# First fixed expert without a split, blocks of up to 32 slots on column quarters, in a two-layer mixture-of-experts encoder

## The chip, the cores and the metric

The kernel runs on one core of one Trainium2 chip. The metric is the device time of one execution of the whole program in microseconds, given as the median of several runs. Engines are named as in the profile: PE is TensorE's matmul, PEld its weight load, DVE is VectorE, ACT is ScalarE, POOL is GpSimd, SP is SyncE, which issues most DMAs.

## The reference

Two post-norm residual layers over 1024 tokens of width 1024. Each layer has a mixer (attention) and then the mixture of experts that the change is about: 4 groups of 8 experts, each token goes to its best group and there to its best two experts.

```python
for i in range(DEPTH):                      # DEPTH = 2
    m = even_mixer(x, ...) if i % 2 == 0 else odd_mixer(x, ...)
    x = layer_norm(DN_ALPHA * x + m, ln1_g[i], ln1_b[i])
    f = hier_moe(x, w_router_group[i], ..., w_gate[i], w_up[i], w_down[i])
    x = layer_norm(DN_ALPHA * x + f, ln2_g[i], ln2_b[i])

# in hier_moe, for the tokens xb of an expert e, w their gates:
hdn = jax.nn.silu(xb @ w1[e]) * (xb @ w3[e])      # 1024 -> 512, twice
y = (hdn @ w2[e]) * w[:, None]                    # 512 -> 1024
```

All is float32.

## The kernel before

**Experts in an order.** Each layer works through 32 experts one after the other (`moe`, the loop over `s`; position `p` in `ex.order`). Positions 0 and 1 are "fixed": experts 0 and 1, whatever their load, so that their weights can be loaded before the router has chosen (`NFIX = 2`). The other 30 are ranked by load, and `ROOM` gives each rank `r` its slots: ranks 0 to 3 ("big") a block of 128 slots and a remainder of 48, 40, 32 and 16; ranks 4 to 13 ("mid") one block of up to 128; ranks 14 to 29 ("light") 64 down to 24 slots. Fixed experts are ranks 30 and 31, 128 slots each. `light(p)` tells whether a position is of the light kind. In the order, rank 2 stands at position 18, rank 3 at 24, and the four light ranks with 32 or 24 slots at 27, 29, 30 and 31, the end.

**Two kinds of block.** A 128-slot block is computed with split operands: every weight piece (128x1024, half of a 1 MB load) is split into `hi` (ACT, line 2052) and a remainder `lo` (DVE, line 2056, or for the two fixed experts often POOL, line 2054), and each product is three matmuls (`mm3`, lines 169 to 171). Twelve pieces make an expert; five pairs of buffers hold them (`PIECES`). `fill` splits up to `AHEAD` = 3 pieces beyond the one in use; line 825 calls `ex.fill(3)` already during the output projection of the mixer. A 64-slot block takes the loaded weights as they are: `pair` (line 1148) issues two matmuls with 64 stationary columns each, gate and up (or the two halves of down), on the two column halves of the array (line 1151). The trace has two matmul records for each such float32 matmul.

**One stage `s`.** For `i` in 0 to 7 gate and up of expert `s`, then for `i` in 8 to 11 down of expert `s - 1`. In between stand: `deliver(s - 2)` (gate times result plus the gathered token, line 1203, DVE), `turn_hidden(s - 1)` (transposes of the hidden values, line 1181; for 64-slot blocks also silu and the product, lines 1188 and 1189), `scatter` and `gather` (indirect DMAs from POOL, lines 1209 and 1120), and at `i == TURN` (6) `turn(s + 1)`, the transposes of the next expert's tokens (lines 1133 to 1142). In stage 0 one step of `route_rest` (slot tables from one-hot matmuls, lines 1023 to 1062) follows each `i`; the rest of it, `decode` (lines 1071 to 1081) and `gather(2)` come at `i == 0` of stage 1.

**Loads.** Each expert is six loads of 1 MB, in the order of `flow`, into a ring of nine buffers and one of two. `load` issues them on SP; a load waits until the buffer's last reader is done. `follow` (called from stage 1 on) issues as many as there are freed buffers. The first twelve loads (the two fixed experts) go out before and during the routing. PE, ACT, DVE and POOL run in program order; only SP's order is left to the framework's scheduler.

Of the kernel before, what the change touches and what calls it, by code (L numbers as in the profile page):

```python
# [43 lines left out]

POOL_LO_FIRST, POOL_LO_FIRST2 = (2, 4, 5, 7, 8, 10), (0, 2, 4, 6, 8, 10)
# [91 lines left out]
class Kernel:  # L137
# [605 lines left out]
    def out_project(self, layer, ws, x, o_tile):  # L743
# [5 lines left out]
        with ExitStack() as st:  # L749
# [46 lines left out]
            for t in range(NT):  # L796
# [27 lines left out]
                if t == NT - 1:  # L824
                    ex.fill(3)
# [259 lines left out]
    def blocks(self, r):  # L1085

        if r < NBIG:
            return [(r, P, P), (NE + r, 64, ROOM[r] - P)]
        return [(r, P if r < NMID or r >= NE - NFIX else 64, ROOM[r])]

    def moe(self, layer, ahead):
# [3 lines left out]
        with ExitStack() as st:  # L1095
# [16 lines left out]
            def slot(p, b, n):  # L1112
                return [x[0:n, b:b + 1] for x in self.slots]
            gx, cnt = {}, [0]

            def gather(p):
                for b, _, n in self.blocks(order[p]):
                    x = xgs[cnt[0] % XGS]
                    cnt[0] += 1
                    nc.gpsimd.indirect_dma_start(out=x[0:n], out_offset=None, in_=self.x1_dram,  # L1120
                                                 in_offset=bass.IndirectOffsetOnAxis(ap=self.first[:, p:p + 1] if p < NFIX else slot(p, b, n)[0], axis=0),
                                                 bounds_check=S - 1, oob_is_err=False)
                    gx[b] = x
# [4 lines left out]
            def turn(p):  # L1128
                for b, n, _ in self.blocks(order[p]):
                    if n < P:  # L1130
                        pt = flat(psT.tile([P, 4, P], F32, name="tp", tag="tp")).rearrange("p (c s) -> p c s", c=NC)
                        for c in range(NC):
                            nc.tensor.transpose(pt[:, c], gx[b][0:n, c::NC], self.ident[0:n, 0:n])  # L1133
                        xts[b] = pr.tile([P, NC, 64], F32, name="xs", bufs=3)
                        nc.scalar.activation(xts[b], pt, AF.Copy)  # L1135
                        continue
                    hi, lo = xts[b] = pr.tile([P, NC, P], F32R, name="xh"), pr.tile([P, NC, P], F32R, name="xl")
                    for g in range(2):
                        pt = psT.tile([P, 4, P], F32, name="tp", tag="tp")
                        for j in range(4):  # L1140
                            c = 4 * g + j
                            nc.tensor.transpose(pt[:, j, 0:n], gx[b][0:n, c::NC], self.ident[0:n, 0:n])
                        self.split(hi[:, 4 * g:4 * g + 4], lo[:, 4 * g:4 * g + 4], pt[:, :, 0:n])
# [4 lines left out]
            def pair(out, x, c, ws, start, stop):  # L1148

                for i, w in enumerate(ws):  # L1150
                    mm(out[64 * i:64 * i + 64], x[:, c], w, start=start, stop=stop, tile_position=(0, 64 * i))  # L1151

            def gate_up(s, b, c):
                j, z = divmod(c, 4)
                pair(gu[b], xts[b], c, [ex.raws[s, j][:, z], ex.raws[s, 2 + j][:, z]], c == 0, c == NC - 1)

            def down(s, b, c):
                w = ex.raws[s, 4 + c // 2][:, c % 2]
                pair(ys[b], hts[b], c, [w[:, 0:512], w[:, 512:1024]], c == 0, c == 3)
# [17 lines left out]
            def turn_hidden(p):  # L1177
                for b, n, _ in self.blocks(order[p]):
                    pt = psT.tile([P, 4, P], F32, name="tp", tag="tp")
                    for j in range(4):  # L1180
                        nc.tensor.transpose(pt[:, j], hs[b][:, j::4], self.ident)
                    if n == P:
                        hts[b] = [pr.tile([P, 4, P], F32R, name="hh"), pr.tile([P, 4, P], F32R, name="hl")]
                        self.split(hts[b][0], hts[b][1], pt)
                    else:

                        h = hts[b] = pr.tile([P, 4, 64], F32, name="hs", bufs=3)
                        nc.scalar.activation(h, pt[:, :, 0:64], AF.Silu)
                        nc.vector.tensor_tensor(h, h, pt[:, :, 64:128], op=OP.mult)
# [3 lines left out]
            def deliver(p):  # L1193

                todo = []
                for b, n, _ in self.blocks(order[p]):
                    y = ys.pop(b)
                    x = yos[b] = gx.pop(b)
                    gate = slot(p, b, n)[2]
                    for i in range(2):  # L1200
                        out = y[64 * i:64 * i + 64] if n < P else y[i]
                        todo.append(lambda x=x[0:n, 512 * i:512 * i + 512], y=out, gate=gate:
                                    nc.vector.scalar_tensor_tensor(x, y, gate, x, op0=OP.mult, op1=OP.add))  # L1203
                return todo

            def scatter(p, which=(0, 1)):
                for b, _, n in [x for i, x in enumerate(self.blocks(order[p])) if i in which]:
                    yo = yos.pop(b)
                    nc.gpsimd.indirect_dma_start(out=self.y_dram, out_offset=bass.IndirectOffsetOnAxis(ap=slot(p, b, n)[1], axis=0),  # L1209
                                                 in_=yo[0:n], in_offset=None, bounds_check=2 * S - 1, oob_is_err=False)  # L1210

            rest = self.route_rest(c1, pr, psT_as_rt(psm), xgs[-2:])
            over = self.overflow_tables(c1, pr)
            gather(0)
# [3 lines left out]
            for s in range(NE + 1):  # L1218
                if s < NE:
# [5 lines left out]
                    for i in range(8):  # L1225
                        ex.fill((s, i), AHEAD)
                        for b, n, _ in bs:
# [7 lines left out]
                            elif len(bs) == 1:  # L1235
                                gate_up(s, b, i)
                                if i % 4 == 3:
# [7 lines left out]
                        if s:  # L1245
                            ex.follow()
# [17 lines left out]
                        if i == TURN and s + 1 < NE:  # L1264
                            turn(s + 1)
                            if s:
                                for p in range(min(s + 2 + (s > 28), NE), min(s + 3 + (s >= 28), NE)):
                                    gather(p)
# [7 lines left out]
                if s:  # L1276
# [5 lines left out]
                    for i in range(8, 12):  # L1282
# [3 lines left out]
                        if i == 10 and s == NE - 1:  # L1286
                            turn_hidden(s)
                        for b, n, _ in bs:
# [5 lines left out]
                            elif len(bs) == 1:  # L1294
                                down(s - 1, b, i - 8)
                                if i % 2:
# [643 lines left out]
class Experts:  # L1940
# [3 lines left out]
    def __init__(self, k, layer, side):  # L1944
# [18 lines left out]
        for q in range(NE + 1):  # L1963
            self.flow += [(q, j) for j in (0, 2, 1, 3)] if q < NE else []
            self.flow += [(q - 1, j) for j in range(4, 6)] if q and q != NFIX else []
            self.flow += [(q, j) for j in range(4, 6)] if q == NFIX - 1 else []
        self.static = 6 * NFIX
        self.piece_flow, self.place, self.limit = [], {}, {}
        for q in range(NE + 1):
            for p, parts in ((q, range(8)), (q - 1, range(8, 12))):  # L1970
                for i in parts if 0 <= p < NE else ():
# [3 lines left out]
                    if i < 8 and self.light(p):  # L1975
# [9 lines left out]
    def light(self, p):  # L1985

        return p < NE and NMID <= self.order[p] < NE - NFIX
# [52 lines left out]
    def fill(self, key, ahead=0):  # L2040
# [4 lines left out]
        while self.filled < upto:  # L2045
# [75 lines left out]
```

## Time and profile before

| | |
|---|---|
| median of three runs | 2590.37 us (2587.05 to 2594.7) |
| profiled execution | 2594.29 us, its span 2592.5 us |
| PE busy | 2391.4 us (92%) |
| DVE busy | 1618.8 us (62%) |
| ACT busy | 1232.0 us (48%) |
| POOL busy | 545.6 us (21%) |
| DMA | 582 MB, 225 GB/s on average |

The two expert stages take the stretches from about 775 to 1358 us and from about 1959 to 2540 us. Shares over the whole span are means of stages with different limits, so the expert stages are read by themselves, in windows and in the order of time.

### The profile page before, as it was taken

To read this page: it belongs to the slowest core of one execution; us is meant where nothing else is said; L and a number is where in the kernel's file an instruction comes from. 1 tells how busy PE (TensorE), PEld (TensorE's weight loads), DVE (VectorE), ACT (ScalarE), POOL (GpSimd) and SP (SyncE) were. 2 spreads that over 40 slices of the span, in tenths; PEclk is the share of its full clock that TensorE was granted. 3 is DMA by queue.
4 is the path that set the end of the run, shared out by engine and by line. 5 is a ranking of instruction groups with operands and counts; after the bars stand their busy time and mean duration, and the time that the engine had idled before them with its cause. 6 is when DMAs were issued, how large, how long until landed. Compare 5 with 4: busy or idle time off the path is not lost. (4 is left out here: it accounts for less than half of the span.)

```text
span 2592.5 us, 34453 instructions
## 1 busy us (share of the span) xinstructions
PE 2391.4 (92%) x11900; PEld 1730.1 (67%) x11900; DVE 1618.8 (62%) x2885; ACT 1232.0 (48%) x2101; POOL 545.6 (21%) x539
## 2 busy tenths in 40 slices
PE   8999999999978999999996999998896999999991
PEld 8776777887765656656545878887784655655650
DVE  4328867887577665656535357676577675656546
ACT  3227866777234534445324356666323544434433
POOL 0007742332015111111111022223013210111112
PEclk9999999999988989999998999999997999999996
DMA  4104312002535898999996564455724799999996
GB/s 150 33 26 93 82 42 70 1 1 73 201 138 191 334 386 346 397 399 406 366 379 231 160 140 128 117 134 160 261 106 168 308 396 358 402 387 413 361 394 243
DMA packets 179753, 582.11 MB, mean 225 GB/s; under 512 B 32728, under 2 KB 91112, under 8 KB 128632
## 3 DMA queue, kind: packets, MB, share of 16 engines
q1 hardware_dynamic: 165880, 546.29, 58.3%
q0 software_dynamic: 13696, 33.58, 3.6%
q8 instruction: 96, 1.57, 0.3%
q14 instruction: 81, 0.66, 0.1%
HBM read 518.61 MB, written 56.05 MB: 222 GB/s over the span
## 5 line engine op out<-in xcount | busy, mean ns | idle before, releaser
L2056 DVE TENSOR_TENSOR lo<-raw,hi 128x1024 fp32r<-128x1024 f32 x358 | 426.5, 1235 | 86.8 <-ACT hi L2052 82.4
L2052 ACT ACTIVATE hi<-raw 128x1024 fp32r<-128x1024 f32 x384 | 389.0, 1058 | 41.6 <-PE hy L171 41.2
L1151 PE MATMUL hy<-raw,xs 128*64 128x512 f32 x1280 | 297.5, 599 | 0.0
L1209 POOL DMA_INDIRECT y_scratch<-xg,msi x72 | 71.6, 994 | 881.8 <-DVE xg L1203 800.1
L170 PE MATMUL hy<-lo,xh 128*128 128x512 f32 x512 | 206.9, 404 | 17.2 <-DVE lo L2056 17.1
L169 PE MATMUL hy<-hi,xh 128*128 128x512 f32 x512 | 214.1, 418 | 0.0
L171 PE MATMUL hy<-hi,xl 128*128 128x512 f32 x512 | 205.6, 402 | 0.0
L1203 DVE SCALAR_TENSOR_TENSOR xg<-hy,mgate,xg 64x512 f32<-64x512 f32 (+1 forms) x144 | 104.3, 746 | 133.8 <-PE hy L1151 116.4
L1151 PEld LDWEIGHTS hy<-raw,xs 128*64 128x64 f32 x1280 | 84.6, 136 | 149.9 <-issue 142.3
L1151 PE MATMUL hy<-raw,hs 128*64 128x512 f32 x640 | 148.7, 603 | 0.0
L163 DVE TENSOR_TENSOR pl<-tp,ph 128x512 fp32r<-128x512 f32 x192 | 129.9, 681 | 23.7 <-ACT ph L162 23.7
L162 ACT ACTIVATE ph<-tp 128x512 fp32r<-128x512 f32 x192 | 112.3, 595 | 40.6 <-PE tp L666 23.3
L2054 POOL TENSOR_TENSOR lo<-raw,hi 128x1024 fp32r<-128x1024 f32 x26 | 64.6, 2506 | 306.5 <-ACT hi L2052 302.1
L169 PE MATMUL o<-whi,xh 128*128 128x512 f32 (+1 forms) x320 | 125.7, 393 | 3.4 <-ACT whi L162 3.3
L170 PE MATMUL o<-wlo,xh 128*128 128x512 f32 (+1 forms) x320 | 124.9, 390 | 1.5 <-DVE wlo L163 1.3
L170 PEld LDWEIGHTS hy<-lo,xh 128*128 128x128 f32 x512 | 99.8, 195 | 39.3 <-DVE lo L2056 20.3
L171 PE MATMUL o<-whi,xl 128*128 128x512 f32 (+1 forms) x320 | 123.8, 387 | 0.1
L169 PEld LDWEIGHTS hy<-hi,xh 128*128 128x128 f32 x512 | 99.7, 195 | 34.3 <-ACT hi L2052 6.5
L1135 ACT ACTIVATE xs<-tp 128x512 f32<-128x512 f32 x40 | 23.9, 598 | 197.3 <-PE tp L1133 197.3
L1170 DVE TENSOR_TENSOR hg<-hg,hy 128x512 f32<-128x512 f32 x32 | 22.0, 688 | 149.9 <-PE hy L171 133.9
L1737 POOL TENSOR_SCALAR e<-e,sm 128x288 f32<-128x288 f32 (+1 forms) x128 | 68.7, 549 | 219.8 <-DVE sm L1736 196.9
L171 PEld LDWEIGHTS hy<-hi,xl 128*128 128x128 f32 x512 | 99.6, 194 | 22.3 <-DVE xl L154 0.5
(426 smaller groups left out, 5678.5 us busy)
## 6 DMA issues: line engine op xcount, KB each, us to landing
raw<-in_w_gate_dram SPq DMA_DIRECT2D x128, 1024.0 KB
raw<-in_w_up_dram SPq DMA_DIRECT2D x128, 1024.0 KB
raw<-in_w_down_dram SPq DMA_DIRECT2D x128, 1024.0 KB
y<-y_scratch SPq DMA_DIRECT2D x14, 1024.0 KB
v_scratch<-vst SPq DMA_DIRECT2D x32, 256.0 KB
raw<-in_odd_w_qkv_dram SPq DMA_DIRECT2D x16, 512.0 KB
vw<-v_scratch SPq DMA_DIRECT2D x16, 512.0 KB
x_scratch<-z SPq DMA_DIRECT2D x14, 512.0 KB
```

The costliest lines, as they stand in the source:

```text
L162: nc.scalar.activation(hi, src, AF.Copy)
L163: return lambda: nc.vector.tensor_tensor(lo, src, as32(hi), op=OP.subtract)
L169: mm(out, l[0], r[0], start=start, stop=False)
L170: mm(out, l[0], r[1], start=False, stop=False)
L171: mm(out, l[1], r[0], start=False, stop=stop)
L1151: mm(out[64 * i:64 * i + 64], x[:, c], w, start=start, stop=stop, tile_position=(0, 64 * i))
L1203: nc.vector.scalar_tensor_tensor(x, y, gate, x, op0=OP.mult, op1=OP.add))
L1209: nc.gpsimd.indirect_dma_start(out=self.y_dram, out_offset=bass.IndirectOffsetOnAxis(ap=slot(p, b, n)[1], axis=0), in_=yo[0:n], in_offset= ...
L1737: nc.gpsimd.tensor_scalar(e, e, sm[:, 2:3], 1.0, op0=OP.mult, op1=OP.mult)
L2052: nc.scalar.activation(hi, src, AF.Copy)
L2054: nc.gpsimd.tensor_tensor(lo, src, as32(hi), op=OP.subtract)
L2056: nc.vector.tensor_tensor(lo, src, as32(hi), op=OP.subtract)
```

## The change

- The first fixed expert (rank 30, position 0) is no longer split: its 128 slots become two blocks of 64 (`blocks`), which use the loaded weights by `pair`; it counts as light in the plan of pieces. It is still gathered as one unit of 128 (`units`).
- Blocks of up to 32 slots (the remainders of ranks 2 and 3, and the light ranks with 32 and 24 slots: six blocks in each layer) are computed on column quarters: `pair` issues four matmuls with 32 stationary columns, two of the contraction's chunks at once. `turn_hidden` adds the two partial sums of gate and up; `deliver` adds two partial sums of down with one instruction each, four instead of two.
- No remainder is computed on POOL any more; all go to DVE. The early `ex.fill(3)` in the output projection is gone.
- Gate and up loads (1, 0) and (1, 2) of the second fixed expert move to the front of `flow`; `follow` is called in stage 0 too; in stage 1 `turn(2)` and its gather move from `i == 6` to `i == 10`.

```diff
-POOL_LO_FIRST, POOL_LO_FIRST2 = (2, 4, 5, 7, 8, 10), (0, 2, 4, 6, 8, 10)
...
-                if t == NT - 1:
-                    ex.fill(3)
...
+        small = lambda n: 32 if n <= 32 else 64
         if r < NBIG:
-            return [(r, P, P), (NE + r, 64, ROOM[r] - P)]
-        return [(r, P if r < NMID or r >= NE - NFIX else 64, ROOM[r])]
+            return [(r, P, 0), (NE + r, small(ROOM[r] - P), 0)]
+        if r == NE - NFIX:
+            return [(r, 64, 0), (2 * NE, 64, 64)]
+        return [(r, P if r < NMID or r > NE - NFIX else small(ROOM[r]), 0)]
+
+    def units(self, r):
+
+        if r < NBIG:
+            return [(r, P, [r]), (NE + r, ROOM[r] - P, [NE + r])]
+        return [(r, ROOM[r], [r, 2 * NE] if r == NE - NFIX else [r])]
...
-                            nc.tensor.transpose(pt[:, c], gx[b][0:n, c::NC], self.ident[0:n, 0:n])
-                        xts[b] = pr.tile([P, NC, 64], F32, name="xs", bufs=3)
-                        nc.scalar.activation(xts[b], pt, AF.Copy)
+                            nc.tensor.transpose(pt[:, c, 0:n], gx[b][at:at + n, c::NC], self.ident[at:at + n, at:at + n])
+                        xts[b] = pr.tile([P, NC, 64], F32, name="xs", bufs=3)[:, :, 0:n]
+                        nc.scalar.activation(xts[b], pt[:, :, 0:n], AF.Copy)
...
-            def pair(out, x, c, ws, start, stop):
-
-                for i, w in enumerate(ws):
-                    mm(out[64 * i:64 * i + 64], x[:, c], w, start=start, stop=stop, tile_position=(0, 64 * i))
+            def pair(out, x, c, ws, nk):
+                n = x.shape[-1]
+                q = P // n // 2
+                if c % q < q - 1:
+                    return
+                for i in range(2):
+                    for z in range(q):
+                        k = c + 1 - q + z
+                        at = n * (q * i + z)
+                        mm(out[at:at + n], x[:, k], ws(k)[i], start=k == z, stop=k == nk - q + z, tile_position=(0, at))
...
-                        h = hts[b] = pr.tile([P, 4, 64], F32, name="hs", bufs=3)
-                        nc.scalar.activation(h, pt[:, :, 0:64], AF.Silu)
-                        nc.vector.tensor_tensor(h, h, pt[:, :, 64:128], op=OP.mult)
+                        h = pr.tile([P, 4, 64], F32, name="hs", bufs=3)
+                        g, u = pt[:, :, 0:64], pt[:, :, 64:128]
+                        if n == 32:
+                            even, odd = [pt.rearrange("p j (i z s) -> p j i z s", i=2, z=2)[:, :, :, z] for z in range(2)]
+                            t = pr.tile([P, 4, 2, 32], F32, name="hz", bufs=1)
+                            nc.scalar.activation(t, odd, AF.Copy)
+                            nc.vector.tensor_tensor(t, t, even, op=OP.add)
+                            h, g, u = h[:, :, 0:32], t[:, :, 0], t[:, :, 1]
+                        hts[b] = h
+                        nc.scalar.activation(h, g, AF.Silu)
+                        nc.vector.tensor_tensor(h, h, u, op=OP.mult)
...
-                        out = y[64 * i:64 * i + 64] if n < P else y[i]
-                        todo.append(lambda x=x[0:n, 512 * i:512 * i + 512], y=out, gate=gate:
-                                    nc.vector.scalar_tensor_tensor(x, y, gate, x, op0=OP.mult, op1=OP.add))
+                        outs = [y[i]] if n == P else [y[a:a + n] for a in range(64 * i, 64 * i + 64, n)]
+                        for out in outs:
+                            todo.append(lambda x=x[:, 512 * i:512 * i + 512], y=out, gate=gate:
+                                        nc.vector.scalar_tensor_tensor(x, y, gate, x, op0=OP.mult, op1=OP.add))
...
-                        if s:
-                            ex.follow()
+                        ex.follow()
...
-                        if i == TURN and s + 1 < NE:
-                            turn(s + 1)
...
+                        if i == TURN and s != 1 and s + 1 < NE:
+                            tokens(s)
...
+                        if i == 10 and s == 1:
+                            tokens(s)
...
+        first = [(1, 0), (1, 2)]
+        self.flow = first + [x for x in self.flow if x not in first]
...
-        return p < NE and NMID <= self.order[p] < NE - NFIX
+        return p < NE and NMID <= self.order[p] <= NE - NFIX
...
-            if i in (POOL_LO_FIRST if p < 1 else POOL_LO_FIRST2 if p < 2 else ()) or 2 <= self.filled <= AHEAD:
-                nc.gpsimd.tensor_tensor(lo, src, as32(hi), op=OP.subtract)
-            else:
-                nc.vector.tensor_tensor(lo, src, as32(hi), op=OP.subtract)
+            nc.vector.tensor_tensor(lo, src, as32(hi), op=OP.subtract)
```

`tokens(s)` is `turn(s + 1)` and, from stage 1 on, the gathers that followed it at `i == TURN` before.

## Rows read from the trace of the kernel before

**Rows 1.** Window of 20 us: busy PE, PEld, DVE, ACT, POOL, granted clock, DMA share, GB/s

```profile
780.00:800.00 20.00, 13.62 (x50) 9.21 (x50) 19.53 (x39) 5.17 (x5) 9.15 (x4) 0.74 0.35 111
```

**Rows 2.** Timeline of PE, start of layer 0's experts: start, us, line, op, [idle <-releaser]

```profile
777.47 0.79 PE L169 MATMUL hy<-hi,xh 128*128 128x512 f32 x1
...
791.59 0.32 PE L1055 MATMUL hy<-rhs,xg 128*128 128x160 bf16 x1 [6.38 <-DVE xg L1049]
...
803.95 0.24 PE L1055 MATMUL hy<-rhs,xg 128*128 128x160 bf16 x1
...
806.84 0.50 PE L169 MATMUL hy<-hi,xh 128*128 128x512 f32 x1
...
818.43 0.80 PE L170 MATMUL hy<-lo,xh 128*128 128x512 f32 x1 [4.75 <-DVE lo L2056]
```

**Rows 3.** Timeline of DVE in the same stretch

```profile
771.42 0.16 DVE L968 TENSOR_TENSOR gm<-rtm,rtm 128x8 f32<-128x8 f32 x1
...
784.55 2.34 DVE L1037 CAST r<-pcol 128x8 bf16<-128x8 f32 x1
...
795.09 0.17 DVE L1037 CAST r<-pcol 128x8 bf16<-128x8 f32 x1
...
809.07 7.58 DVE L1081 TENSOR_SCALAR mgate<-mgate 128x36 f32<-128x36 f32 x1
```

**Rows 4.** Timeline of POOL in the same stretch

```profile
779.30 9.85 POOL L2054 TENSOR_TENSOR lo<-raw,hi 128x1024 fp32r<-128x1024 f32 x4 [9.27 <-ACT hi L2052]
...
809.54 7.06 POOL L2054 TENSOR_TENSOR lo<-raw,hi 128x1024 fp32r<-128x1024 f32 x3
```

**Rows 5.** Timeline of PE: 24 products of a split block, then pairs, then transposes

```profile
825.89 0.39 PE L169 MATMUL hy<-hi,hh 128*128 128x512 f32 x1
...
831.42 1.94 PE L1151 MATMUL hy<-raw,xs 128*64 128x512 f32 x8
...
854.20 3.65 PE L1151 MATMUL hy<-raw,xs 128*64 128x512 f32 x16
857.79 0.50 PE L169 MATMUL hy<-hi,xh 128*128 128x512 f32 x1
...
882.17 1.10 PE L1133 MATMUL tp<-ident,xg 64*128 64x64 f32 x8
```

**Rows 6.** Groups by line: busy us, mean ns, idle before them

```profile
L2056 DVE TENSOR_TENSOR lo<-raw,hi 128x1024 fp32r<-128x1024 f32 x358 | 426.5, 1235 | 86.8 <-ACT hi L2052 82.4 <-issue 0.4
L2052 ACT ACTIVATE hi<-raw 128x1024 fp32r<-128x1024 f32 x384 | 389.0, 1058 | 41.6 <-PE hy L171 41.2
```

**Rows 7.** Timeline of PE, start of layer 1's experts: first product, first pair

```profile
1961.20 0.79 PE L169 MATMUL hy<-hi,xh 128*128 128x512 f32 x1
...
2015.52 1.94 PE L1151 MATMUL hy<-raw,xs 128*64 128x512 f32 x8
```

**Rows 8.** Longer windows, columns as in Rows 1, first of layer 0, then of layer 1

```profile
1140.00:1220.00 80.00, 79.02 (x374) 45.62 (x370) 48.73 (x53) 36.31 (x48) 12.96 (x12) 1.00 1.01 406
1220.00:1260.00 40.00, 40.00 (x187) 23.12 (x186) 20.73 (x23) 17.66 (x24) 4.40 (x4) 1.00 0.90 347
...
1320.00:1340.00 20.00, 20.00 (x98) 10.25 (x96) 6.47 (x7) 5.25 (x8) 0.95 (x1) 1.00 0.97 378
...
2340.00:2400.00 60.00, 59.18 (x277) 36.12 (x276) 35.99 (x39) 26.30 (x33) 11.07 (x10) 1.00 1.01 414
2400.00:2440.00 40.00, 39.84 (x190) 23.26 (x192) 19.70 (x22) 16.35 (x22) 4.40 (x4) 1.00 0.85 331
...
2500.00:2520.00 20.00, 20.00 (x97) 10.06 (x96) 7.27 (x8) 5.85 (x8) 1.50 (x2) 1.00 0.92 355
```

**Rows 9.** Timeline of SP, layer 0's last loads (issue begins, last ends, count)

```profile
1335.43 6.10 SPq L2076 DMA_DIRECT2D raw<-in_w_down_dram  x4
```

**Rows 10.** Timeline, end of layer 0's experts: last pairs, last two deliveries

```profile
1352.90 5.37 PE L1151 MATMUL hy<-raw,hs 128*64 128x512 f32 x24
...
1358.32 1.51 DVE L1203 SCALAR_TENSOR_TENSOR xg<-hy,mgate,xg 64x512 f32<-64x512 f32 x2 [1.92 <-PE hy L1151]
```

More of the change, by code (lines that the diff above doesn't have):

```diff
@@ L1110, in moe, with slot @@
             order, pieces = ex.order, ex.pieces
-            def slot(p, b, n):
-                return [x[0:n, b:b + 1] for x in self.slots]
-            gx, cnt = {}, [0]
+            def slot(b, n, at=0):
+                return [x[at:at + n, b:b + 1] for x in self.slots]
+            gx, cols, cnt = {}, {}, [0]
             def gather(p):
-                for b, _, n in self.blocks(order[p]):
+                for b, n, keys in self.units(order[p]):
                     x = xgs[cnt[0] % XGS]
@@ L1120, in gather @@
                     nc.gpsimd.indirect_dma_start(out=x[0:n], out_offset=None, in_=self.x1_dram,
-                                                 in_offset=bass.IndirectOffsetOnAxis(ap=self.first[:, p:p + 1] if p < NFIX else slot(p, b, n)[0], axis=0),
+                                                 in_offset=bass.IndirectOffsetOnAxis(ap=self.first[:, p:p + 1] if p < NFIX else slot(b, n)[0], axis=0),
                                                  bounds_check=S - 1, oob_is_err=False)
-                    gx[b] = x
+                    for k in keys:
+                        gx[k], cols[k] = x, b
             xts, hts, gu = {}, {}, {}
             def turn(p):
-                for b, n, _ in self.blocks(order[p]):
+                for b, n, at in self.blocks(order[p]):
                     if n < P:
@@ L1213, in moe, with tokens @@
             over = self.overflow_tables(c1, pr)
+            def tokens(s):
+                turn(s + 1)
+                if s:
+                    for p in range(min(s + 2 + (s > 28), NE), min(s + 3 + (s >= 28), NE)):
+                        gather(p)
             gather(0)
@@ L1293, in moe @@
                                     product(ys[b][z], hts[b], i - 8, (hi[:, sl], lo[:, sl]), i == 8, i == 11)
-                            elif len(bs) == 1:
+                            elif bs[0][1] < P:
                                 down(s - 1, b, i - 8)
-                                if i % 2:
+                                if i % 2 and b == bs[-1][0]:
                                     ex.free(s - 1, i // 2)
@@ L1974, in __init__ @@
                         self.piece_flow.append((p, i))
-                    if i < 8 and self.light(p):
+                    if i < 8 and p and self.light(p):
                         self.limit[p, i] = n + max(0, i - 3)
```

24 lines of the change are left out of this document (10 added, 14 removed).

## The prediction

> **What bounds the kernel now.** The change touches only the two expert stages, so I read these by themselves, in the order of time. First the windows: they show which engine is full and at what clock. From stage 8 or so to the end PE is busy for all of a window (79.0 of 80 us, 40.0 of 40) at a granted clock of 1.00 [rows 8], so PE sets the pace there. At the same time the DMA engines are near their own limit: 406 GB/s over 80 us of layer 0 and 414 over 60 us of layer 1, with only a few windows below (347, 378, 331, 355) [rows 8]. A second bound thus lies close behind PE: a faster PE soon waits for weights.
>
> The beginning of a stage looks different. From 780 to 800 us PE is busy for 13.6 of 20 us at clock 0.74, DVE is full (19.5) and the DMA engines idle (111 GB/s) [rows 1]. The timeline of PE names the two waits: 6.38 us for the one-hot tables of the routing, and 4.75 us for a `lo` piece, both on DVE [rows 2]. Why is DVE late? Its timeline shows instructions on 8 elements a partition that take 2.34 us, where the same instruction takes 0.17 us in the second round, and a scaling of 36 elements that takes 7.58 us [rows 3]. During exactly these, POOL runs its remainders: four in a row from 779.30 for 9.85 us, three from 809.54 for 7.06 us [rows 4]. DVE's short instructions end when a POOL instruction ends: POOL shuts DVE out. After each wait PE also starts at the lower of its two clock levels.
>
> **The change part by part.**
>
> *Unit prices.* 24 products of a split block take 825.89 to 831.42, 0.230 us each. 16 records of pairs take 854.20 to 857.79, 0.224 us each [rows 5]. A split block of 72 products is 16.6 us of PE; a 64-slot block of 48 records is 10.8 us.
>
> *The start of a stage.* From the first product (777.47) to the first pair of expert 2 (831.42) is 53.95 us [rows 2, 5]. Full-clock work in it: the first expert 16.6, the second's gate and up 48 x 0.230 = 11.0, the two groups of table matmuls 2 x 2.9 (803.95 to 806.84) [rows 2], twenty transposes at 1.1 per eight [rows 5], 2.8. Sum 36.2. The other 17.8 are the 11.1 of the two waits and 6.7 of slow clock. After the change the first expert is two unsplit blocks, 96 x 0.224 = 21.5 instead of 16.6; four more transposes cost 0.6; the sum is 41.7. Do the waits go? Without POOL, DVE does four pieces first (4 x 1.24 [rows 6], from about 772 [rows 3] to 777) and then a round of tables whose instructions are 0.2 to 1.5 us, some 6 us: done at about 783. PE has five double steps of gate and up (5 x 4 records x 2 blocks x 0.224 = 9 us) before it needs them, until about 787. So the tables are hidden with 4 us to spare, and if that cover were gone each us would come back as a wait. The 7.58 us scaling falls to a few tenths. No piece is split in stage 0, since the four of the second expert exist already and the next wait for stage 1; there ACT and DVE need 1.06 and 1.24 us a piece [rows 6] against 1.4 us of PE, so they keep up. I leave 1 us of slow clock at the start: 42.7 against 53.95 gives 11.2 us in layer 0. In layer 1 the stretch is 54.3 us [rows 7]; there the four `hi` (4.2 us of ACT [rows 6], done in the projection before) may hold up the first token copies, as the gather lands sooner; bounds 0 and 2, I take 1: 10.6 us. Bounds for each layer are 8 (half of the slow clock stays, and one more us of wait) and 13.
>
> *What this triggers.* `follow` in stage 0 fills freed buffers earlier, at a time when DMA carries 111 GB/s [rows 1]: free. Loads (1, 0) and (1, 2) are already there in both orders. From stage 2 on, PE and the loads that it releases shift together, so the gain is kept. `turn(2)` moved behind most of stage 1 has `gather(2)` issued some 12 us before it; I cost it at nothing, and its cover is the second expert's gate and up. The removed `fill(3)` took ACT and DVE in a stretch where both wait for PE: nothing. The moved remainders cost DVE 13 x 1.24 us a layer, less the five DVE pieces of the first expert, beside other work.
>
> *Column quarters.* Six blocks per layer. The trace has no quarter. The nearest row is the pair: two column halves of the array run beside each other, 16 records in 3.59 us, each streaming 512 columns [rows 5]. If four quarters run beside each other as the two halves do, a group of four records takes what two take now, and a block 5.4 instead of 10.8 us: 32 us of PE a layer. From the other side, no gain at all (four records in two turns), or a loss (below). I take the full gain, as two halves already run together.
>
> The rule that speaks against it: rows show 512 columns taken in every 0.224 to 0.230 us both with whole-array products and with pairs [rows 5], and nothing quicker anywhere. The Trainium skill ("TensorE: Matmul & The Clock Gate", Part 2, on the drain) gives PE two read ports, one of which feeds the streaming operand; by that, four streams would take turns, a block would stay at 10.8 us and the sum would be 2572 (rival A). The same page (Part 3) reports three column tiles of 32 at 2.38 times one; by that the gain would be most of mine. No run here shows either yet.
>
> *What of the 32 us reaches the end.* The blocks stand at positions 18, 24, 27, 29, 30 and 31. With PE ahead, loads must come faster than they do. What the DMA engines left unused: in layer 0, 40 us at 347 instead of 406 GB/s is 5.8 us, 20 us at 378 is 1.4; together 7.2. In layer 1, 40 us at 331 instead of 414 is 8.0, 20 at 355 is 2.9; together 10.9 [rows 8]. Then the wait of landed weights: the last four loads are issued from 1335.4 to 1341.5 [rows 9]; 4.2 MB at 406 GB/s are 10.3 us, so they land by 1345.8 at the earliest; the last is first used at 1352.90 + 16 x 0.224 = 1356.5 [rows 10]. A PE that waits for it recovers between 0 and 10.6 us; I take 4.5, as the DMA queue isn't empty then. The last group itself is 0.9 us shorter. Against that, the last deliveries are four instead of two of 0.75 us behind the last matmul [rows 10]: 1.5 us more on the path. The added copy and sum in `turn_hidden` lie ahead of the last loads and are hidden by them; without that cover, 1 us. Layer 0: 7.2 + 4.5 + 0.9 - 1.5 = 11.1. Layer 1: 14.8. Both are well under 32, so the loads, not PE, decide; that a quarter costs somewhat more than a fourth would hardly matter.
>
> *Sum.* 11.2 + 10.6 + 11.1 + 14.8 = 47.7 us. Against the profiled execution of 2594.3 that is 2546.6. That execution stands 3.9 above the median of the runs (2590.4); from the median I get 2542.7, and forecast **2542 us**.
>
> **The rivals.**
>
> A. *Quarters run no faster than halves.* For: nothing in the rows passes 512 columns per 0.22 us [rows 5]. Against: float32 pairs show that column parts stream on their own. The start still gains; the ends lose the 1.5 us: 2590.4 - 21.8 + 3 = 2572.
>
> B. *A new wait takes the place of the old ones at the start.* The second block's hidden values need a buffer that the second table holds until its matmuls run in stage 1, and `turn(2)` may meet a gather that isn't there; ACT, and behind it the next `hi`, would queue. Each would cost a few us of wait and as much of slow clock, as the 4.75 us wait did [rows 2]. At 6 us a layer: 2554.
>
> C. *Slower: each quarter takes a turn of its own.* If two quarters can't stream beside each other, a record keeps the array for the 0.45 us that a pair of records takes now; a block is 48 x 0.45 = 21.5 instead of 10.8 us. Twelve such blocks on a full PE add 128 us: 2572 + 128 = 2700. It decides from the point where a block costs (21.8 - 3) / 12 = 1.6 us more than now, 12.4 us; below that the start pays for it. Against it: the halves do run together [rows 5].
>
> D. *Loads keep up.* If the DMA engines carry more than the 414 GB/s of the fullest window [rows 8] or the wait of landed weights is the full 10.6 us, more of the 32 us arrives; with half of what is left: 2522.
>
> **How the numbers follow.** Forecast 0.60, A 0.17, B 0.10, C 0.08, D 0.05. The range should reach from D to A: 2522 to 2573; it leaves out C and the odd case, and holds the bounds of the start (8 to 13 a layer) and of the landed weights (0 to 10.6 a layer). A measurement here tells some 0.3%, 8 us, from no change. Faster by more: forecast, D, and all but a little of A and B, 0.87. Within: A and B together, 0.04. Slower: C and what I don't see, 0.09.
>
> **What would show it.** No POOL `lo` and no DVE instruction of 2 us on a few elements in the first 40 us; no wait of PE on the tables or on `lo` there; first pair of expert 2 some 42 to 43 us after the first matmul of expert 0 (step one). Records of quarters at about 0.11 us each (step two); 0.22 is A, 0.45 is C. In the last 60 us of each stage, PE waiting for loads, DMA above 400 GB/s to the end (step three). If PE stays full there and DMA doesn't, the third step is wrong. A wait on ACT or the gather in stage 1 is B.

## The result and the profile after

The changed kernel takes **2549.56 us** (median of 4 runs, 2545.34 to 2551.8) against 2592.53 us for the kernel before on the same occasions: a ratio of 0.9835, 95% interval 0.9812 to 0.9858, or 43.0 us less. The forecast was 2542 us, 48 us less, with a range of 2522 to 2573. The profiled execution of the changed kernel took 2551.09 us (span 2549.3), 43.2 less than that of the kernel before.

The start of layer 0's experts, timeline of PE of the changed kernel (start, us, line, operation, count, idle before and its releaser); it answers to [rows 2, 5]:

```profile
774.41 1.65 PE L1139 MATMUL tp<-ident,xg 64*128 64x64 f32 x16 [3.26 <-DMA xg<-x_scratch,fgi]
776.26 10.72 PE L1165 MATMUL hy<-raw,xs 128*64 128x512 f32 x40 [0.20 <-ACT xs L1141]
786.91 0.24 PE L1051 MATMUL hy<-rhs,xg 128*128 128x160 bf16 x1
...
819.41 1.89 PE L1165 MATMUL hy<-raw,xs 128*64 128x512 f32 x8
```

The table matmuls at 786.91 follow the pairs without a wait, where there were 6.38 us of it. From the first product (776.26) to the first pair of expert 2 (819.41) are 43.15 us; before it was 53.95. In layer 1 the same two stand here, 44.22 us apart instead of 54.32 [rows 7]:

```profile
1941.47 11.79 PE L1165 MATMUL hy<-raw,xs 128*64 128x512 f32 x40 [0.67 <-ACT xs L1141]
...
1985.69 1.89 PE L1165 MATMUL hy<-raw,xs 128*64 128x512 f32 x8
```

Why the tables are early is in the timeline of DVE (to [rows 3]). The instruction on 8 elements takes 0.17 instead of 2.34 us:

```profile
772.91 4.63 DVE L2083 TENSOR_TENSOR lo<-raw,hi 128x1024 fp32r<-128x1024 f32 x4 [1.26 <-ACT hi L2082]
...
779.45 0.17 DVE L1033 CAST r<-pcol 128x8 bf16<-128x8 f32 x1
...
781.85 1.52 DVE L1045 TENSOR_SCALAR xg<-iotab,po 128x192 bf16<-128x192 bf16 x8
```

Now the quarters and the end of layer 0, timeline of PE. Sixteen records on 32 columns take 1290.12 to 1291.86, 0.109 us each; the individual starts come in fours, 0.43 us from one four to the next. Towards the end PE stands between them, and the releaser is a load almost every time:

```profile
1290.12 1.92 PE L1165 MATMUL hy<-raw,hs 128*32 128x512 f32 x16
1291.86 1.04 PE L1165 MATMUL hy<-raw,xs 128*32 128x512 f32 x8
...
1314.84 1.06 PE L1165 MATMUL hy<-raw,hs 128*32 128x512 f32 x8 [0.48 <-DMA raw<-in_w_down_dram]
1317.05 1.07 PE L1165 MATMUL hy<-raw,hs 128*32 128x512 f32 x8 [1.14 <-DMA raw<-in_w_down_dram]
1319.64 1.92 PE L1165 MATMUL hy<-raw,xs 128*32 128x512 f32 x4 [1.53 <-DMA raw<-in_w_gate_dram]
...
1337.35 1.94 PE L1165 MATMUL hy<-raw,hs 128*32 128x512 f32 x8 [1.37 <-DMA raw<-in_w_down_dram]
```

The windows of those 60 us (columns as in [rows 8]) show PE falling from 18.5 to 14.6 us of 20 and its granted clock to 0.76, while the DMA engines carry 387 to 420 GB/s:

```profile
1280.00:1300.00 20.00, 18.48 (x107) 10.51 (x106) 10.63 (x15) 6.38 (x10) 4.87 (x4) 1.00 1.01 397
1300.00:1320.00 20.00, 14.85 (x86) 7.10 (x87) 8.45 (x11) 5.08 (x9) 0.94 (x1) 0.99 1.01 420
1320.00:1340.00 20.00, 14.56 (x72) 3.10 (x68) 6.26 (x11) 1.98 (x5) 1.77 (x2) 0.76 0.98 387
```

**Where the 43.2 us went**, by the distance between the same events in the two traces (us that the changed kernel is ahead; a position is taken at the transposes of its hidden values):

| event | ahead | gained since the line above |
|---|---|---|
| first product, layer 0 | 1.2 | 1.2 |
| first pair of expert 2 | 12.0 | 10.8 |
| position 17 (last without quarters) | 10.6 | -1.4 (slow clock after the stall of stage 8) |
| position 29 | 24.7 | 14.1 |
| last matmul of layer 0's experts | 19.0 | -5.7 |
| first product, layer 1 | 19.7 | 0.7 |
| first pair of expert 2 | 29.8 | 10.1 |
| position 17 (last without quarters) | 31.5 | 1.7 (a slow clock here in the kernel before alone) |
| position 28 | 47.2 | 15.7 |
| last matmul of layer 1's experts | 44.0 | -3.2 |
| end of the span | 43.2 | -0.8 |

So two halves: the starts, 20.9 us, and what the quarters bring, which rises to 14.1 and 15.7 us and is partly given back in the last three stages. The two entries on the clock hang on how long the lower clock lasted behind a wait that both kernels have: layer 0 loses 1.4 us so, layer 1 gains 1.7. In layer 1 a wait of 0.98 us for tokens, which both kernels have, is followed by a clock of 0.91 in the kernel before (window 2280 to 2300) and by 1.00 in the changed one.

### The profile page after: what moved, and what is told of

It is laid out like the page before. It is cut to its first block, busy times and chain, and to the rows that moved or that the text cites. A ratio compares the mean times of both kernels' runs of the same rounds, so it can differ in the third digit from the quotient of the medians.

```text
span 2549.3 us, 34566 instructions
## 1 busy us (share of the span) xinstructions
PE 2352.0 (92%) x11972; PEld 1691.2 (66%) x11972; DVE 1601.5 (63%) x2923; ACT 1209.1 (47%) x2093; POOL 484.6 (19%) x513
## 5 line engine op out<-in xcount | busy, mean ns | idle before, releaser
L2082 ACT ACTIVATE hi<-raw 128x1024 fp32r<-128x1024 f32 x360 | 363.7, 1057 | 43.2 <-PE hy L169 34.1
L1165 PE MATMUL hy<-raw,xs 128*64 128x512 f32 (+1 forms) x1408 | 302.3, 615 | 7.0 <-DMA raw<-in_w_up_dram 3.1
L1226 DVE SCALAR_TENSOR_TENSOR xg<-hy,mgate,xg 128x512 f32<-128x512 f32 (+2 forms) x172 | 125.3, 745 | 129.0 <-PE hy L1165 115.8
L167 PE MATMUL hy<-hi,xh 128*128 128x512 f32 x480 | 197.1, 411 | 0.0
L1165 PEld LDWEIGHTS hy<-raw,xs 128*64 128x64 f32 (+1 forms) x1408 | 80.4, 132 | 159.4 <-issue 137.0
L1165 PE MATMUL hy<-raw,hs 128*64 128x512 f32 (+1 forms) x704 | 144.8, 608 | 11.7 <-DMA raw<-in_w_down_dram 10.2
L161 DVE TENSOR_TENSOR pt<-tp,pt 96x384 fp32r<-96x384 f32 (+1 forms) x128 | 65.2, 549 | 70.9 <-ACT pt L160 69.5
L151 ACT ACTIVATE hh<-tp 128x512 fp32r<-128x512 f32 x30 | 17.9, 597 | 185.5 <-PE tp L1194 185.5
L657 POOL TENSOR_SCALAR e<-e,sm 128x1024 f32<-128x1024 f32 x64 | 72.1, 1126 | 177.5 <-DVE sm L656 111.9
L1141 ACT ACTIVATE xs<-tp 128x512 f32<-128x512 f32 (+1 forms) x44 | 23.4, 537 | 173.0 <-PE tp L1139 173.0
## 6 DMA issues: line engine op xcount, KB each, us to landing
raw<-in_w_down_dram SPq DMA_DIRECT2D x128, 1024.0 KB, 14.6
```

The source lines that it names most:

```text
L161: return lambda: nc.vector.tensor_tensor(lo, src, as32(hi), op=OP.subtract)
L167: mm(out, l[0], r[0], start=start, stop=False)
L657: nc.gpsimd.tensor_scalar(e, e, sm[:, 3:4], 1.0, op0=OP.mult, op1=OP.mult)
L1165: mm(out[at:at + n], x[:, k], ws(k)[i], start=k == z, stop=k == nk - q + z, tile_position=(0, at))
L2082: nc.scalar.activation(hi, src, AF.Copy)
```

## The experiments

All times are medians; ratios are against the kernel before, run on the same chip on the same occasions.

**The two parts by themselves.** First the changed kernel without quarters:

```
-        small = lambda n: 32 if n <= 32 else 64
+        small = lambda n: 64
```

> The changed kernel, but blocks of up to 32 slots run as two column halves of 64 again. If the start and the quarters are two separate gains, the start keeps some 11 us in each layer, the six blocks of a layer cost 10.8 us again, and PE has no wait for loads over 1 us in the last 60 us of a stage: 2570 us, within 4. If the loads already set the end in the kernel before, the quarters were worth little and this stays below 2556. If every microsecond that the quarters save on PE reached the end, it is 65 us slower than the changed kernel, 2614.

Measured: 2571.06 us, ratio 0.9909 (0.9891 to 0.9927), and PE stays full in the windows of the end, as before:

```profile
1300.00:1320.00 20.00, 20.00 (x95) 10.52 (x94) 8.04 (x9) 6.56 (x9) 0.91 (x1) 1.00 0.97 366
1320.00:1340.00 20.00, 20.00 (x97) 7.60 (x98) 3.33 (x6) 1.96 (x4) 1.81 (x2) 1.00 1.01 410
```

The start is worth 0.0091 x 2592.5 = 23.6 us by itself. The quarters bring the rest, (0.9909 - 0.9835) x 2592.5 = 19 us; each interval is about 5 us wide on either side, so 19 is known to some 7 or 8.

Then the kernel before, with only the remainders moved from POOL to DVE:

```
-            if i in (POOL_LO_FIRST if p < 1 else ...) or 2 <= self.filled <= AHEAD:
-                nc.gpsimd.tensor_tensor(lo, src, as32(hi), op=OP.subtract)
-            else:
-                nc.vector.tensor_tensor(lo, src, as32(hi), op=OP.subtract)
+            nc.vector.tensor_tensor(lo, src, as32(hi), op=OP.subtract)
```

> The kernel before with one edit: the remainders that POOL took are on DVE; the first expert stays split. If POOL's subtractions shutting DVE out are the whole cause of the stalls at the start, both waits (6.4 and 4.8 us) nearly go although DVE has ten more pieces of 1.24 us there: about 8 us a layer, 2576 us. If the cause is DVE's own load, PE waits for remainders and tables about as long as before, with the waits in other places: under 3 us a layer, 2586 us or more, and taking the split out of the first expert was needed.

Measured: 2576.31 us, ratio 0.9935 (0.991 to 0.996), the first outcome. The wait for the tables is down to 0.42 us, that for a remainder is gone, and from the first product to the first pair are 44.5 us (44.8 in layer 1). A new wait of 2.8 us, for the tokens' remainder `xl` of the second expert on DVE, stands in each layer:

```profile
782.41 0.79 PE L169 MATMUL hy<-hi,xh 128*128 128x512 f32 x1
...
790.89 0.24 PE L1055 MATMUL hy<-rhs,xg 128*128 128x160 bf16 x1 [0.42 <-DVE xg L1049]
...
802.36 0.79 PE L171 MATMUL hy<-hi,xl 128*128 128x512 f32 x1 [2.82 <-DVE xl L154]
...
826.93 1.94 PE L1151 MATMUL hy<-raw,xs 128*64 128x512 f32 x8
```

Taking POOL out is most of the start: 9.4 and 9.5 of the 10.8 and 10.1 us by these distances, and 0.0065 of 0.0091, 17 of 23.6 us, by the medians. That the first expert isn't split any more adds 0.9935 - 0.9909 = 0.0026 with everything else of the change but the quarters, within the two intervals: not told from nothing.

**Is it POOL that shuts DVE out?** The changed kernel with POOL work that nobody needs, behind the first two gathers; first six additions:

```
             gather(1)
+            for _ in range(6):
+                nc.gpsimd.tensor_tensor(xgs[3], xgs[3], xgs[3], op=OP.add)
             ex.fill(AHEAD)
```

> The changed kernel plus six additions on POOL behind the first two gathers of each layer (a buffer of zeros added to itself, 128 x 1024; nobody waits for the result until a much later gather). If POOL's two-operand instructions shut DVE out, DVE's instructions on 8 elements take 2 us and more again while they run, PE waits 3 us or more for the tables and drops to the lower clock: 6 to 12 us a layer, 2562 to 2574 us. If DVE was late only by its own work, DVE's instructions keep their 0.17 us and the time stays within 4 us of the changed kernel.

Measured: 2554.37 us, ratio 0.9862 (0.9837 to 0.9888); not told from the changed kernel. The expected loss did not come, as POOL ended before DVE reached the short instructions of the tables. The four remainders met it, and before them one instruction on 32 elements (timelines of POOL and DVE):

```profile
769.27 14.35 POOL L1246 TENSOR_TENSOR xg<-xg 128x1024 f32<-128x1024 f32 x6
...
769.00 2.23 DVE L1001 CUSTOM_DVE_ANT_0 room<-sq,room 32x32 f32<-32x32 f32 x1
...
774.54 10.16 DVE L2085 TENSOR_TENSOR lo<-raw,hi 128x1024 fp32r<-128x1024 f32 x4 [1.27 <-ACT hi L2084]
```

The remainders took 10.16 us instead of 4.63, the instruction before them 2.23 instead of 0.17. The same with a multiplication by a constant, one operand from memory:

```
+                nc.gpsimd.tensor_scalar(xgs[3], xgs[3], 1.0, None, op0=OP.mult)
```

> As the run with six additions on POOL, but each is a multiplication of the same buffer by a constant: one operand from memory instead of two. If any work of POOL on that memory shuts DVE out, the result is that of the additions. If it needs two operands, DVE's short instructions stay below 0.5 us and the time is within 4 us of the changed kernel.

Measured: 2553.45 us, ratio 0.9852 (0.9836 to 0.9869). POOL was busy longer and covered the remainders wholly, yet they took 5.47 us, little more than alone:

```profile
767.79 17.86 POOL L1246 TENSOR_SCALAR xg<-xg 128x1024 f32<-128x1024 f32 x6
...
771.78 5.47 DVE L2085 TENSOR_TENSOR lo<-raw,hi 128x1024 fp32r<-128x1024 f32 x4 [1.26 <-ACT hi L2084]
...
780.13 0.89 DVE L1036 TENSOR_TENSOR gr<-ga,r 128x8 f32<-128x8 f32 x1
```

Neither outcome came as it was written: the remainders were hardly held, but two of DVE's ten instructions on 8 elements took 0.79 and 0.89 us, over the 0.5 of the expectation, and the eight that build the tables 3.04 instead of 1.52. The time shows none of it.

The six additions were too early, so there should be more of them (`range(12)`):

> The changed kernel with twelve additions on POOL in place of six. Six took 14.4 us and ended as DVE came to its short instructions; DVE's four remainders took 10.2 instead of 5.5 us in that time and the tables were still early enough. Twelve last some 29 us and cover the tables as well. If POOL shuts DVE out, DVE's instructions on 8 elements now take 2 us or more until about 798 us, PE waits 5 us or more for the tables in both layers, and the time is 2563 to 2575 us. If the effect ends with the large instructions, the time is within 4 us of the run with six.

Measured: 2582.91 us, ratio 0.9964 (0.995 to 0.9977): 33 us more than the changed kernel, more than expected. With POOL busy to 798.7, five of DVE's ten instructions on 8 elements take 1.65 to 1.86 us again, and PE waits 9.5 us in layer 0 (10.0 in layer 1) for the tables:

```profile
771.44 27.24 POOL L1246 TENSOR_TENSOR xg<-xg 128x1024 f32<-128x1024 f32 x12
...
787.00 1.65 DVE L1020 SCALAR_TENSOR_TENSOR ga<-gm,gw 128x8 f32<-128x8 f32 x1
...
792.91 1.86 DVE L1033 CAST r<-pcol 128x8 bf16<-128x8 f32 x1
...
PE hy L1051 <- DVE xg L1045: 9.5, 1, 9.5
```

(The last line is from the table of PE's waits: us in total, times, longest.) The stretch from the first product to the first pair of expert 2 is 56.0 and 55.5 us, longer than before the change; that is 24 of the 33 us, and where the rest arose was not followed. No data hangs on those additions in that stretch, so it is the running of POOL's additions that holds DVE.

**What holds the quarters back?** The forecast said: the loads at the end of a stage, where four short blocks fall in the last five positions. Then another order of the same experts should give the loss back. The smallest first:

```
-        mid, light = list(range(NBIG, NMID)), list(range(NMID, NE - NFIX))
+        mid, light = list(range(NBIG, NMID)), list(range(NMID, NE - NFIX))[::-1]
```

> The changed kernel, with the order of the experts of at most 64 slots turned round: the smallest come first (positions 2, 5, 7, 9), two of 64 slots come last. PE's work is the same. If loads set the end because four short blocks fall in the last five positions, where an expert's six loads take some 15 us and its PE work 7 to 8, the waits for loads at the end go (5.8 us in layer 0 and 3.2 in layer 1 came back there) without new ones at the start, whose loads have an idle queue: 2540 us. If the loads are short everywhere, the waits move to positions 2 to 9 and the time stays at 2550 or grows.

Measured: 2547.88 us, ratio 0.983 (0.9806 to 0.9853): nothing. PE's direct waits for loads fell from 9.7 and 8.0 us to 2.0 and 1.7, but at stage 8 there is a new one of 4.11 us on ACT, which stood 7.49 us behind the sum that a quarter block needs from DVE while DVE was at the overflow tables (timelines of ACT and PE):

```profile
928.21 0.31 ACT L1210 ACTIVATE hs<-hz 128x128 f32<-128x128 f32 x1 [7.49 <-DVE hz L1207]
928.43 2.94 ACT L2082 ACTIVATE hi<-raw 128x1024 fp32r<-128x1024 f32 x3
...
929.52 0.80 PE L167 MATMUL hy<-hi,xh 128*128 128x512 f32 x1 [4.11 <-ACT hi L2082]
```

Two explanations are left: the order didn't help because of that stall, or because the loads are short everywhere. So the overflow tables were spread over stages 8 to 10, in the order of the change and in the turned one:

```
-                        elif s >= 8:
+                        elif s >= 8 and i == 5:
                             next(over, None)
```

> The changed kernel, with the three parts of the overflow tables taken in stages 8, 9 and 10, one each, instead of in the first three steps of stage 8. There PE waits 3.8 us for remainders in each layer and falls to the lower clock. If what the start gained can be had there too, PE's time falls by 5 to 9 us in each layer and the loads follow it: 2536 us. If the loads set the end of the stage whatever happens before, what is gained at stage 8 comes back as waits for loads at the end: 2547 us or more.

> Both edits together: smallest experts first, overflow tables spread over stages 8 to 10. If the two limits (loads at the end, DVE at stage 8) are separate, the gains add: 2528 us. If loads are short through the whole stage, the sum is less than either by 5 us or more: 2536 us or above.

Measured: 2544.49 us, ratio 0.9807 (0.9779 to 0.9836), and 2543.93 us, ratio 0.9803 (0.9778 to 0.9828). Each is 5 to 6 us below the changed kernel, where 13 and 21 were hoped for; their intervals overlap with its own. In the first, against the changed kernel, stage 8 gained 9.3 and 5.7 us (layers 0 and 1) and stage 9 lost 2.7 and 4.5: PE waits there 2.83 us for tokens (`xl`) behind the second part of the tables. In the other, against the run with the smallest first, stage 8 gained 11 in each layer and stage 9 lost 7.7 and 5.6 us; there ACT's next piece waits 4.96 us for a `w_down` load, the tokens queue behind it, and PE waits 8.21 us for them.

Next, the quarters in the middle, between heavy experts, away from both the end of the stage and the overflow tables:

```
+        light = light[:5] + [26, 19, 27, 20, 28, 21, 29] + light[8:12]
         heavy = [r for i in range(NBIG) ...]
```

> The changed kernel, with the four experts of at most 32 slots at positions 13, 17, 21 and 25, between heavy ones, instead of 27, 29, 30 and 31; PE's work is the same. With the smallest first, the waits for loads at the end fell from 9.7 and 8.0 to some 2 us a layer, but ACT stood 7.5 us behind the sum that a quarter block needs from DVE, which was at the overflow tables of stage 8. In the middle there is no such work. If the loads bind only because the short blocks stand together, the waits at the end go without new ones: 2536 us. If the loads are short over the whole stage, waits appear at positions 17 to 26, or ACT waits for loads there: 2547 us or more.

Measured: 2547.63 us, ratio 0.9835 (0.9817 to 0.9852): the second outcome. No direct wait for a load of over 0.4 us is left in layer 0, and new waits of 6.02 and 5.33 us stand at 1097 and 1201 us. In layer 1 the longest such wait is 6.8 us. The chain behind the first, timelines of ACT and PE:

```profile
1091.27 2.01 ACT L2083 ACTIVATE hi<-raw 128x1024 fp32r<-128x1024 f32 x2 [3.30 <-DMA raw<-in_w_down_dram]
1093.92 1.06 ACT L2083 ACTIVATE hi<-raw 128x1024 fp32r<-128x1024 f32 x1 [0.65 <-DMA raw<-in_w_down_dram]
1094.88 1.07 ACT L151 ACTIVATE xh<-tp 128x512 fp32r<-128x512 f32 x2
...
1096.89 1.08 PE L1139 MATMUL tp<-ident,xg 32*128 32x32 f32 x8 [6.02 <-DVE xl L152]
```

ACT waits 3.95 us for weights of the running expert, the next expert's tokens queue behind it on ACT and DVE, and PE waits for those: a wait for loads under another name.

The same order with the overflow tables in stages 9, 11 and 13, and the changed kernel's own order with them there:

> The same order, and the three parts of the overflow tables in stages 9, 11 and 13 (experts without pieces of their own), at the third step, well ahead of the next tokens. If the two limits are separate, the 3.8 us of waits at stage 8 and their slow clock go too, 6 to 9 us a layer: 2522 us. If what is saved at stage 8 comes back as waits for loads: 2535 us or more.

> The changed kernel with its own order and the overflow tables at the third step of stages 9, 11 and 13. Taken at stages 8 to 10, they saved 7.8 and 5.7 us at stage 8, lost 2.7 and 4.5 at stage 9 where the next expert's tokens waited behind them, and the end gave back another 1 to 3 us. If the place was the fault, stage 9 loses nothing: 2538 us. If the loads at the end take back all that comes earlier: 2546 us or more.

Both use

```
-                        elif s >= 8:
+                        elif s in (9, 11, 13) and i == 2:
                             next(over, None)
```

Measured: 2547.09 us, ratio 0.9828 (0.9812 to 0.9845), and 2545.24 us, ratio 0.9818 (0.9801 to 0.9836). The first came out as its second outcome: against the run with the quarters in the middle, stage 8 gained 7.0 and 5.7 us in the traces, the layers from first product to last matmul only 2.7 and -0.3. In the second, stage 9 still loses 1.9 and 4.8 us against the changed kernel: its tables, 946.97 to 949.96, now lie ahead of three remainders and the tokens on DVE, and PE waits 2.88 us as before. So this place was no better, and neither outcome of the second expectation is shown: the end of layer 0 has 10.3 us of direct waits for loads against 9.7 in the changed kernel, and took back nothing that can be told. What the stall of stage 8 is worth stays open.

What six orders and places have in common is one line of the windows. Over 480 us of layer 0, the kernel before:

```profile
860.00:1340.00 480.00, 473.26 (x2184) 283.46 (x2184) 280.18 (x326) 209.94 (x266) 66.79 (x60) 0.99 0.97 380
```

the changed kernel, layer 0 and layer 1:

```profile
860.00:1340.00 480.00, 461.14 (x2211) 273.47 (x2209) 287.00 (x343) 206.41 (x267) 70.00 (x62) 0.97 0.99 389
2020.00:2500.00 480.00, 459.86 (x2240) 273.40 (x2236) 291.94 (x350) 208.39 (x270) 69.72 (x63) 0.98 0.97 389
```

with the smallest first, and with both edits:

```profile
860.00:1340.00 480.00, 459.28 (x2198) 273.46 (x2197) 287.34 (x344) 206.08 (x266) 69.30 (x63) 0.97 0.99 390
```

```profile
860.00:1340.00 480.00, 460.82 (x2232) 274.75 (x2228) 290.79 (x347) 208.95 (x269) 68.79 (x62) 0.98 1.00 392
```

and with the quarters in the middle:

```profile
860.00:1340.00 480.00, 456.69 (x2212) 273.77 (x2210) 289.35 (x347) 206.91 (x267) 70.67 (x62) 0.98 0.99 390
```

The DMA share is 0.97 to 1.00 over the whole stage, not at its end alone, and the rate 387 to 392 GB/s in every kernel with quarters, in both layers. All these kernels load the same weights, so the rate says little that the time doesn't; the share is the reading that stands by itself. In the changed kernel each window of 20 us from 1000 to 1340 has 0.98 to 1.02. The largest hole in layer 0 is from 940 to 1000 (0.91, 0.90 and the row below), where SP waits up to 11.8 us for a buffer that PE still reads:

```profile
980.00:1000.00 20.00, 20.00 (x98) 10.08 (x96) 3.97 (x6) 4.31 (x7) 1.95 (x2) 1.00 0.68 259
```

The kernel before had 380 and a share of 0.97 with PE at 473 of 480 us: the two engines were already within 2% of each other. If 392 is the most that a stage carries, a faster PE could gain some 480 x (1 - 380/392) = 15 us a layer, wherever its work stands. This is an estimate and not a tight one: the run without quarters, with PE just as full, has 386 in layer 0, which leaves 7, and 380 in layer 1.

**The order of the first loads.** The one line of the change that has not come up yet, undone:

```
-        first = [(1, 0), (1, 2)]
-        self.flow = first + [x for x in self.flow if x not in first]
```

> The changed kernel with the loads of the two fixed experts in their old order; the rest of the change stays. The forecast costed the new order at nothing: the time stays within 4 us of the changed kernel (2546 to 2554 us). If the second expert's first loads landed too late for the four pieces that are now made ahead, PE waits for pieces at the start of both layers by 5 us or more: 2560 us.

Measured: 2550.21 us, ratio 0.9839 (0.9821 to 0.9857). It costs and brings nothing that can be told.

None of the variants is clearly faster than the changed kernel; the lowest, smallest first with the tables spread, has 2543.9 us and an interval that overlaps with its own.

## Why the prediction was right, point by point

**The start: right, in cause and size.** Predicted were 42.7 us from the first product to the first pair of expert 2, measured 43.15 and 44.22; a gain of 11.2 and 10.6 us, measured 10.8 and 10.1. Each of its steps holds: the tables' first round ended at 783.4 and was needed at 786.9 (predicted 783 and 787), no table or remainder is waited for, and DVE keeps up. The run with twelve additions shows the cause: POOL running there brings the waits back, without any data between the two. That the first expert had to lose its split was argued, not shown: the kernel before with POOL alone taken out has 44.5 and 44.8 us, 1.4 and 0.6 more. DVE did the ten more pieces there at the price of the new wait of 2.8 us for `xl`.

**The unit price of quarters: right.** Predicted 0.11 us a record and 5.4 us a block, measured 0.109 us (1.74 us for 16), 5.2 us. At the two heavy positions that hold such a block (18 and 24) PE's passage shortened by 5.1 us each, 3.3 in gate and up and 1.8 in down. The Trainium skill ("TensorE: Matmul & The Clock Gate", Part 2, on the drain) gives PE one read port for the streaming operand, from which rival A took it that four streams take turns and a block keeps its 10.8 us. The trace doesn't agree with taking turns: four streams of 512 columns take 0.43 us together, where two took 0.448 [rows 5]. Rivals A and C are out with it, and D by PE's 9.7 and 8.0 us of waits for loads.

**What of it reaches the end: right in kind, somewhat high, and put in the wrong place.** The sign it named came: over the last 60 us of layer 0's experts PE waits for loads while the DMA engines carry 401 GB/s. Predicted were 12.6 and 16.3 us up to the last matmul (11.1 and 14.8 with the deliveries); measured are 8.4 (from 10.6 to 19.0) and 12.5 (from 31.5 to 44.0) from position 17 on, and 19 us for both layers by the medians against 25.9. That difference is about as large as the error of the 19, so the size is not shown to be wrong. What is off is the term of unused rate from single low windows, with its wait of landed weights, as if the loads were a limit of the last part. The runs point to a limit of the whole stage: moved to the front or the middle, the short blocks lost the waits at the end (9.7 to 2.0 us) and not the time; in the middle the waits came back through ACT's queue. No run took the loads themselves away, so this is argued from shares and waits. Read over the whole stage, the row of the kernel before, 380 GB/s at a share of 0.97, would have put the limit in the right place; as a size its 15 us a layer is no better than the 12.6 and 16.3. In layer 0, 1.5 of the missing 4.2 us are another thing: at position 23 the same wait of 0.98 us for tokens was followed by the lower clock (0.91 in the window from 1200), which it was not in the kernel before.

**The deliveries: priced at 1.5 us a layer, and little of it came.** Four deliveries instead of two do end later behind the last matmul, but the scatter waits for the one before it anyway (timelines of DVE and POOL):

```profile
1339.35 3.06 DVE L1226 SCALAR_TENSOR_TENSOR xg<-hy,mgate,xg 32x512 f32<-32x512 f32 x4 [2.84 <-PE hy L1165]
...
1343.40 0.89 POOL L1232 DMA_INDIRECT y_scratch<-xg,msi  x1 [5.69 <-DMA y_scratch<-xg,msi]
```

PE's next matmul comes 18.44 us after the last of the experts, before 18.70. In layer 1 the rest of the span grew by 0.8 us, so something of the price may stand there.

**What was costed at nothing** was nothing as far as it shows: the order of the loads (its run), `turn(2)` and the second block's buffer (rival B; PE's waits for ACT at the start are 0.2 and 0.7 us, and none is put down to the gather). `follow` in stage 0 had no run of its own. The added copy and sum in `turn_hidden` were costed at nothing under their cover, 1 us without; with the cover gone PE waits 4.1, as the run with the smallest first shows: not by their own length, but because ACT waits in the middle of them for DVE, and pieces queue behind.

**Left open.** How much time the stall at stage 8 holds: each place tried for the tables put another stall of 2.8 us or more one stage later. Why the loads stop at 390 GB/s over a stage, while single windows carry 420, was not tried. Neither was a kernel that loads less, so that PE's own bound with quarters has not been seen, nor one with more buffers for the loads, which might fill the hole from 940 to 1000.

## What to carry to other kernels

Before an engine is made faster, read the second engine over the whole stretch, not in its best and worst windows: with DMA at a share of 0.97, some 3% of the stretch was left to gain here, and no order of the work tried got more. An engine that seems slow on tiny instructions may be held by another one: look at who runs in exactly those microseconds, and test it with work that nobody needs. And when a reorder makes one wait vanish without the time moving, follow the new wait back through every queue; here it ended at the same loads.

## What the runs showed of the hardware that was not expected

- Two-operand additions on POOL double DVE's subtractions (10.16 instead of 4.63 us for four) and make five of ten 8-element instructions of DVE take 1.65 to 1.86 instead of 0.17 us, a cast among them. Multiplications by a constant on POOL, over the same buffer and busy for longer, took the subtractions to 5.47 us only and two of the ten to 0.79 and 0.89. The Trainium skill ("SBUF — State Buffer", section on the two separate sides) has the pair of ports that both share held by one instruction, while the other blocks wholly; the additions agree with that; the subtractions beside the multiplications, which were hardly held, don't.
- Four matmul records on 32 columns each start within 0.02 us of each other, and the next four 0.43 us later; the weights of the next are loaded beside them.
